# The prologue of a fused attention, delta-rule and MLP block: p's products first, three input tiles begun as u arrives, the decay's small operations as a chain

## The chip, the core and the metric

The kernel runs on one core of one Trainium2 chip. Five engines have each a queue of their own and work it off in order: PE (TensorE, matmuls), DVE (VectorE), ACT (ScalarE), POOL (GpSimd) and SP (SyncE, which issues most DMAs). The metric is the device time of one execution in microseconds (us), the median of several.

## What is computed

One transformer block over 512 positions of width 1024, all in float32. The part that matters here is its start: the norm of `x`, the wide projection `proj`, the decay of the gated delta rule, and the product of `p` that is needed only at the end.

```python
def reference(x, p, ...):
    u = rmsnorm(h, pre_mix_norm[i])
    proj = jnp.einsum('btd,de->bte', u, w_in[i])
    (da_q, da_k, da_v, gdn_qkv, gdn_z, gdn_b, gdn_a, gate_a_in, gate_b_in) = jnp.split(proj, splits, axis=-1)
    ...
    beta = jax.nn.sigmoid(gdn_b)
    log_decay = -jnp.exp(gdn_a_log[i]) * jax.nn.softplus(gdn_a + gdn_dt_bias[i])
    o_b = gated_delta_rule(g_q, g_k, g_v, log_decay, beta)    # uses cumsum(log_decay) per chunk
    ...
    e = jnp.einsum('btp,pd->btd', p[i], w_ple[i]) * jax.nn.sigmoid(...)
    return h + rmsnorm(e, ple_norm[i])
```

## The kernel before

Everything lies with channels on the 128 partitions and the 512 positions along the free axis: `x` and `u` are 8 pieces (`KD`) of 128x512. A product is made in three passes from split operands: ACT casts a tile to its high half (`whi`, `u_hi`), DVE or POOL subtracts to get the low half (`wlo`, `u_lo`), and PE adds high times high, high times low and low times high. An output tile of 128 columns is thus 24 matmuls of 128x512: 16 that use `whi` (with `u_hi[k]` and `u_lo[k]` in turn, `dense_steps`), and 8 with `wlo`. Here they are called the 16 and the lows.

**Prologue** (L170 to L199). `p` and two weights of `wple` are loaded, then `x` in 8 pieces. Squares of `x` (ACT, L182) are added up (DVE, L184), `norm_bc` makes the broadcast norm `psr` of the sum with small matmuls, a chain of small DVE operations and one matmul (L145 to L153), and the loop at L188 makes `u`: a scaled piece `ut` (DVE), `u_hi` (ACT), `u_lo` (DVE). The products of `p` are written behind it: 8 tiles of 6 matmuls, each copied from PSUM by ACT (`pp`, L197, two buffers) and sent to DRAM (`pp_d`, L198).

**Decay** (`scalars`, from L215). The tile `ba` holds the 32 columns of beta and decay; `pst` is its transpose, then about twenty operations on 128x64 tiles follow on DVE (`sy`, `sz`, `sp`: softplus by a series) up to `sg`, the log decay. The matmuls `psc` and `psg` sum it along time. `gcr` goes to DRAM and is read back broadcast over the partitions as `dt` (L428).

**Tiles of the projection** (`fill`). A list of output tiles in fixed order: for head 0 the key tile K, the query tile P, the value tiles V0 and V1, then `aq`, `ak`, `av`. Each loads its weights two tiles ahead (three buffers `raw`, two `whi`, two `wlo`). K, P, V0 and V1 go through a convolution (`conv_silu`: ACT, three `acc` operations on DVE at L372, ACT, one more on DVE).

**What sets the order.** Up to L829 a list scheduler orders the instructions of all engines. From `tc.manual_schedule` on, PE's order is that of the program text, which `run` lays out: steps of hand-written chains (`gdn_a`, `gdn_i`, `attn`, ...) are put between the matmuls of `fill`; a chain yields the microseconds of PE work that are to pass before its next step. The other engines are still ordered by the scheduler, with priorities per chain (`URGENT`). An engine waits at the head of its queue until that instruction's operands and buffers are ready. PSUM has three buffers `ps` for output tiles.

Of the kernel before, what the change touches and what calls it, by code (L numbers as in the profile page):

```python
# [37 lines left out]
def hybrid_block(ctx, tc, xT, pT, w1, wba, wa, wb, wo, wup, wdn, wple, wpg, vecs, rows, consts, out):  # L38
# [130 lines left out]

    with pool_("pro", bufs=2) as pool:  # L170
# [15 lines left out]
        for k in range(KD):  # L186
            t = pool.tile([128, T], F32, name="ut")
            V.scalar_tensor_tensor(t, in0=psr, scalar=vec[:, G_MIX + k:G_MIX + k + 1], in1=x[:, k], op0=mult, op1=mult)  # L188
            split(u[0][k], u[1][k], t, V)
        ph = pool.tile([128, 2, T], F32R, name="p_hi", bufs=1)  # L190
        pl = pool.tile([128, 2, T], F32R, name="p_lo", bufs=1)
        split(ph, pl, pr)
        p2 = act(ph), act(pl)
        for d in range(KD):
            ps = newdense(wple[d], p2, 2, G, raw=raws[d] if d < 2 else None)
            pp = pool.tile([128, T], F32, name="pp")
            S.activation(pp, ps, AF.Copy, scale=0.5)  # L197
            nc.sync.dma_start(pp_d[d], pp)  # L198
        nc.sync.dma_start(row, rows.partition_broadcast(128))  # L199
# [15 lines left out]
    def scalars():  # L215
        with pool_("sct", bufs=1) as pool:
            raw = wpool.tile([128, KD, 32], F32, name="ba_raw", tag="raw", bufs=3)
            nc.sync.dma_start(raw, wba)
            wz = [wpool.tile([128, KD, 128], F32R, name="ba_" + n, tag=n) for n in ("whi", "wlo")]
            for w in wz:  # L220
                G.memset(w.bitcast(F32), 0.0)
            split(wz[0][:, :, :32], wz[1][:, :, :32], raw)
            ps = pd.tile([128, T], F32, name="ps")
            dense(ps, wz, u, KD)
            ba = pool.tile([128, T], F32, name="ba")
            S.copy(ba[:32], ps[:32])
            th = pool.tile([16, T], F32, name="th16")
            S.activation(th, ba[:16], AF.Tanh, scale=0.5)
            V.tensor_scalar(th, th, 0.5, 0.5, op0=mult, op1=add)
            nc.sync.dma_start(ber_d, th)  # L230

            pst = pb.tile([128, NC, 32], F32, name="pst", tag="b")
            for c in range(NC):
                PE.matmul(pst[:, c], lhsT=ba[:32, c * 128:(c + 1) * 128], rhs=ident[:32, :32], is_transpose=True)
            S.activation(beta, pst[:, :, 0:16], AF.Tanh, scale=0.5)
            V.tensor_scalar(beta, beta, 0.5, 0.5, op0=mult, op1=add)
            shp = [128, NC, NH]
            y, e, z, z2, p, g = (pool.tile(shp, F32, name=n) for n in ("sy", "se", "sz", "sz2", "sp", "sg"))
            V.tensor_tensor(y, pst[:, :, 16:32], bc(row[:, 0:16], shp, 1), op=add)
            S.activation(e, y, AF.Abs)  # L240
            S.activation(e, e, AF.Exp, scale=-1.0)

            V.tensor_scalar(z, e, 2.0, None, op0=add)
            V.reciprocal(z, z)
            V.tensor_tensor(z, z, e, op=mult)
            V.tensor_tensor(z2, z, z, op=mult)
            V.tensor_scalar(p, z2, 1.0 / 19.0, None, op0=mult)
            for n in (17, 15, 13, 11, 9, 7, 5, 3):
                V.scalar_tensor_tensor(p, in0=p, scalar=1.0 / n, in1=z2, op0=add, op1=mult)
            V.scalar_tensor_tensor(p, in0=p, scalar=1.0, in1=z, op0=add, op1=mult)  # L250
            V.tensor_scalar(y, y, 0.0, None, op0=mx)
            V.scalar_tensor_tensor(y, in0=p, scalar=2.0, in1=y, op0=mult, op1=add)
            ea = pool.tile([128, 16], F32, name="ea")
            S.activation(ea, row[:, 16:32], AF.Exp)
            V.scalar_tensor_tensor(g, in0=y, scalar=-1.0, in1=bc(ea, shp, 1), op0=mult, op1=mult)

            gf = g.rearrange("p c h -> p (c h)")
            psc = pb.tile([128, 2, NC, NH], F32, name="psc", tag="b")
            PE.matmul(psc[:, 0].rearrange("p c h -> p (c h)"), lhsT=tri, rhs=gf, start=True, stop=True)
            PE.matmul(psc[:, 1].rearrange("p c h -> p (c h)"), lhsT=ones, rhs=gf, start=True, stop=True)  # L260
            S.copy(gc_t, psc[:, 0])
            S.activation(eg, psc[:, 0], AF.Exp)
            S.activation(egl, psc[:, 1], AF.Exp)
            V.scalar_tensor_tensor(nbeg, in0=eg, scalar=-1.0, in1=beta, op0=mult, op1=mult)
            V.tensor_tensor(edec, psc[:, 1], gc_t, op=sub)
            S.activation(edec, edec, AF.Exp)
            psg = pb.tile([128, T], F32, name="psg", tag="b")
            for c in range(NC):
                PE.matmul(psg[:16, c * 128:(c + 1) * 128], lhsT=g[:, c], rhs=tri, start=True, stop=True)
            gcr = pool.tile([16, T], F32, name="gcr")  # L270
            S.copy(gcr, psg[:16])
            nc.sync.dma_start(gcr_d, gcr)

            ltmp = pool.tile([128, 64], F32, name="ltmp")
            ls = pool.tile([128, 2], F32, name="ls")
            for i in range(2):
                o = 32 + 128 * i
                V.tensor_tensor(ltmp, row[:, o:o + 64], row[:, o + 64:o + 128], op=mult)
                V.tensor_reduce(ls[:, i:i + 1], ltmp, axis=AX.X, op=add)
            S.activation(ls, ls, AF.Exp)  # L280
            V.scalar_tensor_tensor(nlam, in0=ls[:, 1:2], scalar=-lam0, in1=ls[:, 0:1], op0=add, op1=sub)
# [819 lines left out]
```

## Time and profile before

| | us |
|---|---|
| median of 3 runs (1388.82 to 1392.7) | 1390.83 |
| the profiled execution | 1397.38 |
| its span in the profile | 1395.6 |
| PE busy | 1326.7 (95%) |
| DVE busy | 838.1 (60%) |
| ACT busy | 662.3 (47%) |

The span is one execution as the hardware profiler saw it on the core; the profiled execution's own time stands 6.6 us above the median of the timed runs. The page gives busy times for the whole span, so a stage has to be read from the timeline and from windows of it. A matmul's end is modelled, so the distance between the starts of two matmuls tells their rate better than their durations.

### The profile page before, as it was taken

Reading aid. Unit: us, or ns where it says so; the run is one execution under the profiler, and the core shown is the slowest. Engines: PE = TensorE matmul, PEld = TensorE weight load, DVE = VectorE, ACT = ScalarE, POOL = GpSimd, SP = SyncE. Lnnn points to the kernel's source line nnn. Section 1 sums busy time; section 2 is a strip of 40 time slices with the busy share of each in tenths; the row PEclk is TensorE's granted clock in tenths of the full one; section 3 lists DMA queues with packets and bytes.
Section 4 is the critical chain, followed back from the end, with each engine's and each line's share of the span. In section 5 each row is a group of like instructions: output and inputs, shape, how many; then the busy total and the mean of one; then the engine's idle time right before and its main releaser. Section 6 shows DMA issues by size and latency. Waiting matters only on the chain.

```text
span 1395.6 us, 22459 instructions
## 1 busy us (share of the span) xinstructions
PE 1326.7 (95%) x8402; PEld 1107.5 (79%) x8402; DVE 838.1 (60%) x2155; ACT 662.3 (47%) x1363; POOL 184.5 (13%) x193
## 2 busy tenths in 40 slices
PE   6989999999999999999999999999999999999986
PEld 4867787787777778878888888898888888888985
DVE  6867688777778768776653534368343224433575
ACT  5556575767667476766453412254232223223241
POOL 3111111101111111110000000003320002210341
PEclk9989999999999999999999999999999999999998
DMA  7466655655665566655354743351232233223321
GB/s 249 134 153 132 154 122 135 157 150 126 162 158 139 134 134 166 149 135 143 117 185 167 249 143 113 101 186 46 67 100 91 91 94 102 91 91 108 112 84 61
DMA packets 91117, 182.58 MB, mean 131 GB/s; under 512 B 33632, under 2 KB 40160, under 8 KB 91008
## 3 DMA queue, kind: packets, MB, share of 16 engines
q1 hardware_dynamic: 81648, 147.07, 33.6%
q0 software_dynamic: 9360, 34.08, 13.2%
q8 instruction: 66, 1.08, 0.3%
q14 instruction: 43, 0.35, 0.1%
HBM read 130.19 MB, written 16.84 MB: 105 GB/s over the span
## 4 chain that ended last, share of the span: by engine, by line
PE 73%; DVE 14%; DMA 6%; ACT 3%; SPq 2%; issue 2%; POOL 0%; DVEq 0%; ACTq 0%; POOLq 0%
PE ps L80 64%; DMA dt<-gcr_d 2%; DVE Uq L507 1%; SPq L474 1%; PE psat L80 1%; DVE tmpq L506 1%; DVE h L881 1%; PE psao L80 1%; DMA L<-ld_d 1%; DVE ht L880 1%; DVE acc L372 1%; DMA U<-ud_d 1%; PE psS L80 1%; PE psx L80 1%; DVE nw_t L93 1%
## 5 line engine op out<-in xcount | busy, mean ns | idle before, releaser
L80 PE MATMUL ps<-u_hi,whi 128*128 128x512 f32 (+1 forms) x952 | 385.0, 405 | 0.0
L80 PE MATMUL ps<-u_lo,whi 128*128 128x512 f32 (+1 forms) x952 | 374.8, 395 | 0.0
L80 PE MATMUL ps<-u_hi,wlo 128*128 128x512 f32 (+1 forms) x952 | 250.1, 396 | 0.0
L98 ACT CAST whi<-raw 128x1024 fp32r<-128x1024 f32 (+1 forms) x116 | 116.4, 1005 | 265.4 <-PE ps L80 258.5
L80 PEld LDWEIGHTS ps<-u_hi,whi 128*128 128x128 f32 x952 | 183.2, 192 | 35.4
L80 PEld LDWEIGHTS ps<-u_lo,whi 128*128 128x128 f32 x952 | 183.4, 193 | 33.9
L99 DVE TENSOR_TENSOR wlo<-raw,whi 128x1024 fp32r<-128x1024 f32 x106 | 130.1, 1227 | 126.5 <-PE ps L80 104.2
L80 PEld LDWEIGHTS ps<-u_hi,wlo 128*128 128x128 f32 x952 | 172.6, 189 | 33.7 <-issue 0.2
L117 POOL DMA_DIRECT2D wlo<-raw x65 | 56.2, 864 | 424.5 <-ACT wlo L116 224.6
L80 PE MATMUL ps<-hid_hi,whi 128*128 128x512 f32 x224 | 88.5, 395 | 0.0
L80 PE MATMUL ps<-hid_lo,whi 128*128 128x512 f32 x224 | 88.4, 394 | 0.0
L80 PE MATMUL ps<-brl,whi 128*128 128x512 f32 x208 | 82.1, 394 | 0.0
L80 PE MATMUL ps<-brh,whi 128*128 128x512 f32 x208 | 82.0, 395 | 0.0
L372 DVE SCALAR_TENSOR_TENSOR acc<-ps,cw,acc 128x511 f32<-128x511 f32 (+2 forms) x96 | 71.3, 743 | 8.5 <-ACT acc L369 7.7
L115 ACT CAST whi<-raw 128x1024 fp32r<-128x1024 f32 x65 | 68.0, 1046 | 17.3 <-PE ps L80 17.0
L116 ACT ACTIVATE wlo<-whi 128x1024 fp32r<-128x1024 f32 x65 | 68.6, 1056 | 0.3
L942 POOL TENSOR_TENSOR mr<-mr 128x512 f32<-128x512 f32 (+1 forms) x37 | 39.5, 1070 | 217.9 <-ACT hid_hi L941 217.2
L940 DVE SCALAR_TENSOR_TENSOR mr<-ps,r 128x512 f32<-128x512 f32 (+1 forms) x37 | 22.9, 619 | 74.4 <-PE ps L80 70.7
L80 PE MATMUL ps<-hid_hi,wlo 128*128 128x512 f32 x224 | 56.9, 395 | 0.0
L80 PE MATMUL ps<-brh,wlo 128*128 128x512 f32 x208 | 52.6, 395 | 0.0
L80 PEld LDWEIGHTS ps<-hid_lo,whi 128*128 128x128 f32 x224 | 42.1, 188 | 10.3
L80 PEld LDWEIGHTS ps<-hid_hi,wlo 128*128 128x128 f32 x224 | 42.0, 188 | 10.2
(334 smaller groups left out, 2425.4 us busy)
## 6 DMA issues: line engine op xcount, KB each, us to landing
raw<-w SPq DMA_DIRECT2D x88, 512.0 KB, 3.5
wlo<-raw POOLq DMA_DIRECT2D x65, 512.0 KB, 4.8
...
dt<-gcr_d SPq DMA_DIRECT2D x16, 256.0 KB, 5.1
bB<-ber_d SPq DMA_DIRECT2D x16, 256.0 KB, 5.2
ob_d<-zs SPq DMA_DIRECT2D x16, 256.0 KB, 3.0
```

The lines of the kernel that those rows point to most:

```text
L80: PE.matmul(ps, lhsT=lhsT, rhs=rhs, start=start, stop=stop, **k)
L93: V.tensor_tensor(t, t, h, op=mult)
L98: S.copy(hi, src)
L99: (eng or V).tensor_tensor(lo, src, hi.bitcast(F32), op=sub)
L115: S.copy(whi, raw)
L116: S.activation(wlo, whi.bitcast(F32), AF.Copy, scale=-1.0)
L117: nc.gpsimd.dma_start(wlo, raw, accum_op=add)
L372: V.scalar_tensor_tensor(acc[:, s:], in0=ps[:, :T - s], scalar=cw[:, j, w:w + 1], in1=acc[:, s:], op0=mult, op1=add)
L474: nc.sync.dma_start(dst, Bf[bs, :, bs])
L506: V.tensor_tensor(tv, bc(L[:, j, j + 1:], [128, m, r], 1), bc(Uq[:, :m, j], [128, m, r], 2), op=mult)
L940: V.scalar_tensor_tensor(r[:, :n], in0=ps[:, :n], scalar=0.0, in1=r2[:, sl], op0=mx, op1=mult)
L942: G.tensor_tensor(r[:, :n], r[:, :n], r[:, :n], op=mult)
```

## The change

The prologue is rewritten, and PE's manual order now begins at its top, so that PE follows the program text there too. Weights of `p` are loaded between the pieces of `x`; the products of `p` are placed ahead of the norm (d 0 and 1), ahead of its sum (2 to 4), inside `norm_bc` (5 and 6, by the new argument `between`) and behind it (7). Their low halves are made by DVE instead of POOL. The last square is not added by DVE but summed in PE. The weights of `ba`, K and P are loaded and cast in the prologue, and the loop over k gives each of the three tiles its two matmuls of the 16, the second tile one step of k behind the first, the third two. The lows of `ba` follow at once, those of K and P are given out by `fill` (`begun`, `lows`). `scalars` becomes a chain "C" of three steps with yields of 3 and 9, and its tiles lie in other buffers.

```diff
+    manual = tc.manual_schedule(engines={PE.engine})
+    manual.__enter__()
...
-        raws = [load_raw(wple[d], 2) for d in range(2)]
-        x = pool.tile([128, KD, T], F32, name="x", bufs=1)
-        for k in range(KD):
-            nc.sync.dma_start(x[:, k], xT[:, k])
+        load(0, 1)
+        load(0, 1, 2, wp=False)
+        load(2, 3)
+        load(3, 4, 5, wp=False)
+        load(4, 5)
+        load(6, 7, wp=False)
         nc.sync.dma_start(C, consts)
+        load(6, 7)
         nc.sync.dma_start(vec, vecs)
+        nc.sync.dma_start(ba_raw, wba)
+        firsts = [load_raw(w1[n], KD) for n in (24 + 8, 24)]
+        nc.sync.dma_start(row, rows.partition_broadcast(128))
...
+        def ple(*ds):
+            for d in ds:
+                w = [pool.tile([128, 2, 128], F32R, name="wp" + n, bufs=3) for n in "hl"]
+                split(*w, wr[:, d])
+                ps = pd.tile([128, T], F32, name="ps")
+                dense(ps, w, p2, 2)
+                pp = pool.tile([128, T], F32, name="pp")
+                S.activation(pp, ps, AF.Copy, scale=0.5)
+                nc.sync.dma_start(pp_d[d], pp)
+
+        ple(0, 1)
...
-            if k:
+            if 0 < k < KD - 1:
                 V.tensor_tensor(ss, ss, q, op=add)
-        psr = norm_bc(pool, pt, [ss], EPS)
+        ple(2, 3, 4)
+        psr = norm_bc(pool, pt, [ss, q], EPS, lambda: ple(5, 6))
+        ple(7)
+        S.copy(wz[0][:, :, :32], ba_raw)
+        ws = [wz]
+        for raw in firsts:
+            ws.append([...])
+            S.copy(ws[-1][0], raw)
+        begun = [pd.tile([128, T], F32, name="ps") for _ in ws]
+        for k in range(KD + 2):
+            if k < KD:
+                t = pool.tile([128, T], F32, name="ut")
+                V.scalar_tensor_tensor(t, in0=psr, scalar=vec[:, G_MIX + k:G_MIX + k + 1], in1=x[:, k], op0=mult, op1=mult)
+                split(u[0][k], u[1][k], t, V)
+            for n, (w, ps) in enumerate(zip(ws, begun)):
+                if 0 <= k - n < KD:
+                    for a in u:
+                        mm(ps, w[0][:, k - n], a[k - n], start=k == n and a is u[0], stop=False)
+        V.tensor_tensor(wz[1][:, :, :32], ba_raw, wz[0][:, :, :32].bitcast(F32), op=sub)
+        for raw, w in zip(firsts, ws[1:]):
+            V.tensor_tensor(w[1], raw, w[0].bitcast(F32), op=sub)
...
+    def scalars(_):
+        S.copy(ba[:32], begun[0][:32])
...
+        yield 3.0
+        pst = pb.tile([128, NC, 32], F32, name="pst", tag="b")
+        y, e, z, z2, p, g = (small[:, :, 16 * n:16 * n + 16] for n in range(6))
...
+        yield 9.0
+        PE.matmul(psc[:, 0], lhsT=tri, rhs=gf, start=True, stop=True)
...
+            if i < 2:
+                ps, steps = begun[i + 1], lows(i + 1)
...
+    chains.append([0.0, (), scalars, 0, ("C", 0)])
-        chains.append([0.0, (("V", h, 1), ("A", h - 1)), gdn_a, h, ("A", h)])
+        chains.append([0.0, (("V", h, 1), ("A", h - 1), ("C", 0)), gdn_a, h, ("A", h)])
```

Three places show how instructions move (in brackets what an instruction waits for; DMAHW is a DMA that has landed). On ACT, before, where `u` begins, the pieces of `u` alternate with the copies of p's products:

```order
L98 CAST whi2_274<-raw2_272 128x256 [waits DMAHW3_49,PE_49,Pool_49]
L98 CAST u_hi_90<-ut_160 128x512 [waits DVE_49]
L197 ACTIVATE pp_253<-ps_246 128x512 [waits DMAHW2_49,PE_49]
L98 CAST u_hi_90<-ut_164 128x512 [waits DVE_49]
L98 CAST whi2_290<-raw2_288 128x256 [waits DMAHW4_49,PE_49,Pool_49]
L98 CAST u_hi_90<-ut_168 128x512 [waits DVE_49]
```

Now, at the same place of ACT (`whi8_298` and `whi8_301` are K's and P's weights, `pp_195` to `pp_294` the copies of the products d 2 to 7):

```order
L231 CAST whi8_298<-raw8_121 128x1024 [waits DMAHW4_49]
L231 CAST whi8_301<-raw8_123 128x1024 [waits DMAHW5_49]
L214 ACTIVATE pp_195<-ps_188 128x512 [waits DMAHW7_49]
L214 ACTIVATE pp_209<-ps_202 128x512 [waits DMAHW0_49]
L214 ACTIVATE pp_223<-ps_216 128x512 [waits DMAHW2_49,PE_49,Activation_49]
L214 ACTIVATE pp_264<-ps_257 128x512 [waits DMAHW3_49,PE_49,Activation_49]
L214 ACTIVATE pp_278<-ps_271 128x512 [waits DMAHW5_49,PE_49,Activation_49]
L98 CAST u_hi_90<-ut_307 128x512 [waits DVE_49]
L214 ACTIVATE pp_294<-ps_287 128x512 [waits DMAHW6_49,PE_49,Activation_49]
L98 CAST u_hi_90<-ut_313 128x512 [waits DVE_49]
```

Five copies, each waiting for the write to DRAM of the copy two before it, now stand ahead of the first `u_hi`, and both weight casts ahead of them. On PE, before, `psc` stands in the lows of P (`ps_525`), the second tile of the projection:

```order
L80 MATMUL ps_525<-u_hi_90,wlo8_483 128x512 [waits DVE_49]
L80 MATMUL ps_525<-u_hi_90,wlo8_483 128x512 x5
L259 MATMUL psc_440<-sg_417,C_81 128x64 [waits DVE_49]
L260 MATMUL psc_440<-sg_417,ones_84 128x64
L269 MATMUL psg_449<-C_81,sg_417 16x128 [waits Activation_49]
L269 MATMUL psg_449<-C_81,sg_417 16x128 x3
```

Now it stands in V1 (`ps_563`), the fourth tile, behind 14 of its 16; `ps_626` is `aq`:

```order
L80 MATMUL ps_563<-u_lo_91,whi8_520 128x512
L308 MATMUL psc_578<-small_487,C_81 128x64 [waits DVE_49]
L309 MATMUL psc_578<-small_487,ones_84 128x64
L318 MATMUL psg_587<-C_81,small_487 16x128 [waits Activation_49]
L318 MATMUL psg_587<-C_81,small_487 16x128 x3
L80 MATMUL ps_563<-u_hi_90,whi8_520 128x512
L80 MATMUL ps_563<-u_lo_91,whi8_520 128x512
L80 MATMUL ps_563<-u_hi_90,wlo8_521 128x512 x8
L80 MATMUL ps_626<-u_hi_90,whi8_559 128x512 [waits Activation_49]
```

`psc` moved from the second tile to the fourth; from `aq` on, PE's order is the same as before to the end of the program. On DVE, before, the end of the decay's operations stands among the convolution of K (`acc_512`):

```order
L249 SCALAR_TENSOR_TENSOR sp_416<-sp_416,sz2_415 128x64 [waits DVE_49]
L372 SCALAR_TENSOR_TENSOR acc_512<-ps_486,cw_329,acc_512 128x510 [waits DVE_49]
L249 SCALAR_TENSOR_TENSOR sp_416<-sp_416,sz2_415 128x64 [waits DVE_49]
L372 SCALAR_TENSOR_TENSOR acc_512<-ps_486,cw_329,acc_512 128x509 [waits DVE_49]
L249 SCALAR_TENSOR_TENSOR sp_416<-sp_416,sz2_415 128x64 [waits DVE_49] x2
L250 SCALAR_TENSOR_TENSOR sp_416<-sp_416,sz_414 128x64 [waits DVE_49]
L252 SCALAR_TENSOR_TENSOR sy_412<-sp_416,sy_412 128x64 [waits DVE_49]
L255 SCALAR_TENSOR_TENSOR sg_417<-sy_412,ea_437 128x64 [waits DVE_49]
```

Now it stands among and behind that of V0 (`acc_550`), the third tile, and behind the low half of `aq`'s weights (`wlo8_560`); `small_487` holds all the decay's tiles, and L303 writes the log decay:

```order
L424 SCALAR_TENSOR_TENSOR acc_550<-ps_524,cw_406,acc_550 128x510 [waits DVE_49]
L297 SCALAR_TENSOR_TENSOR small_487<-small_487 128x4x16 [waits DVE_49]
L424 SCALAR_TENSOR_TENSOR acc_550<-ps_524,cw_406,acc_550 128x509 [waits DVE_49]
L297 SCALAR_TENSOR_TENSOR small_487<-small_487 128x4x16 [waits DVE_49]
L99 TENSOR_TENSOR wlo8_560<-raw8_557,whi8_559 128x1024 [waits DMAHW7_49,PE_49]
L297 SCALAR_TENSOR_TENSOR small_487<-small_487 128x4x16 [waits DVE_49]
L426 SCALAR_TENSOR_TENSOR vraw0_549<-vraw0_549,acc_550 128x512 [waits DMAHW3_49,DMAHW6_49,DMAHW1_49,Activation_49]
L297 SCALAR_TENSOR_TENSOR small_487<-small_487 128x4x16 [waits DVE_49]
L298 SCALAR_TENSOR_TENSOR small_487<-small_487 128x4x16 [waits DVE_49]
L300 SCALAR_TENSOR_TENSOR small_487<-small_487 128x4x16 [waits DVE_49]
L303 SCALAR_TENSOR_TENSOR small_487<-small_487 128x4x16 [waits DVE_49]
```

What moved is the last third of the decay's operations: from between K's convolution steps to between and behind those of V0.

## Rows read from the trace of the kernel before

**Rows 1.** Windows: busy us (PE, PEld, DVE, ACT, POOL), granted TensorE clock, DMA share, GB/s.
```profile
40.00:50.00 10.00, 10.00 (x50) 7.94 (x49) 8.80 (x25) 5.41 (x12) 0.00 (x0) 1.00 0.28 102
50.00:60.00 10.00, 10.00 (x45) 8.28 (x45) 8.17 (x14) 3.60 (x7) 1.51 (x1) 1.00 0.67 212
```
**Rows 2.** Chain of waits, two pieces: start, us, what.
```profile
27.62 2.10 DMA pp_d<-pp
...
48.87 12.01 PE ps L80 x52
```
**Rows 3.** Timeline of u's production: start, us, engine, line, operation [idle before <-releaser].
```profile
21.54 0.75 DVE L188 SCALAR_TENSOR_TENSOR ut<-psr,vec,x 128x512 f32<-128x512 f32 x1 [1.22 <-PE psr L153]
...
27.74 0.68 DVE L99 TENSOR_TENSOR u_lo<-ut,u_hi 128x512 fp32r<-128x512 f32 x1
...
29.13 0.68 DVE L99 TENSOR_TENSOR u_lo<-ut,u_hi 128x512 fp32r<-128x512 f32 x1
...
30.22 0.50 PE L80 MATMUL ps<-u_hi,ba_whi 128*128 128x512 f32 x1 [2.19 <-ACT ba_whi L98]
...
35.07 0.50 PE L80 MATMUL ps<-u_lo,ba_whi 128*128 128x512 f32 x1
```
**Rows 4.** DMA issues of four short stretches: KB each, us from issue to landing.
```profile
x<-xT SPq DMA_DIRECT2D x1, 256.0 KB, 7.0
...
raw<-wple SPq DMA_DIRECT2D x1, 128.0 KB, 4.8
...
pp_d<-pp SPq DMA_DIRECT2D x1, 256.0 KB, 2.0
...
pp_d<-pp SPq DMA_DIRECT2D x1, 256.0 KB, 4.0
```
**Rows 5.** Issues of the last x (its line: ns min/median/max, first to last) and of that weight.
```profile
L176 SPq DMA_DIRECT2D x<-xT x8: 431/432/923, 2.1 to 5.4; - x8
...
9.04 0.33 SPq L106 DMA_DIRECT2D raw<-wple  x1
```
**Rows 6.** Timeline of DVE and PE around the end of the decay's operations.
```profile
42.40 1.23 DVE L99 TENSOR_TENSOR wlo<-raw,whi 128x1024 fp32r<-128x1024 f32 x1
...
43.55 0.22 DVE L249 SCALAR_TENSOR_TENSOR sp<-sp,sz 128x64 f32<-128x64 f32 x1
43.68 0.74 DVE L372 SCALAR_TENSOR_TENSOR acc<-ps,cw,acc 128x511 f32<-128x511 f32 x1
...
44.34 0.21 DVE L249 SCALAR_TENSOR_TENSOR sp<-sp,sz 128x64 f32<-128x64 f32 x1
...
46.95 0.23 DVE L255 SCALAR_TENSOR_TENSOR sg<-sy,ea 128x64 f32<-128x64 f32 x1
...
47.23 0.43 PE L259 MATMUL psc<-sg,C 128*128 128x64 f32 x2
...
48.80 0.73 PE L80 MATMUL ps<-u_hi,wlo 128*128 128x512 f32 x2
```
**Rows 7.** Timeline: psk in aq, the second bB of head 0, the first psx.
```profile
60.72 0.60 PE L80 MATMUL psk<-C,kq 128*128 128x128 f32 x4
...
62.90 1.29 POOL L433 TENSOR_TENSOR bB<-bB,dt 128x512 f32<-128x512 f32 x1 [1.42 <-ACT dt L432]
...
70.75 0.28 PE L80 MATMUL psx<-kqh 128*128 128x256 f32 x1
```
**Rows 8.** Timeline of PE behind a wait of 3.47 us.
```profile
99.10 0.80 PE L80 MATMUL psao<-vt,aT 128*128 128x128 f32 x2 [3.47 <-ACT aT L736]
...
100.55 0.63 PE L80 MATMUL ps<-u_hi,whi 128*128 128x512 f32 x1
100.97 0.63 PE L80 MATMUL ps<-u_lo,whi 128*128 128x512 f32 x1
```
**Rows 9.** Windows around that wait, columns as in rows 1.
```profile
98.00:100.00 2.00, 0.90 (x3) 0.90 (x4) 1.90 (x9) 2.00 (x4) 0.00 (x0) 0.50 0.23 86
...
104.00:106.00 2.00, 2.00 (x12) 1.74 (x11) 1.00 (x4) 0.29 (x1) 0.00 (x0) 0.93 0.71 131
```

More of the change, by code (lines that the diff above doesn't have):

```diff
@@ L136, in dense_steps, with norm_bc @@
                 yield
-    def norm_bc(pool, pp, sss, eps):
+    def norm_bc(pool, pp, sss, eps, between=None):
         n = sss[0].shape[1] // 128
@@ L151, in norm_bc @@
         V.tensor_tensor(dg, bc(ident, [128, n, 128], 1), bc(r, [128, n, 128], 2), op=mult)
+        if between:
+            between()
         psr = pp.tile([128, 128 * n], F32, name="psr", tag="t")
@@ L167, in hybrid_block, with load @@
     u = (act(upool.tile([128, KD, T], F32R, name="u_hi")), act(upool.tile([128, KD, T], F32R, name="u_lo")))
+    manual = tc.manual_schedule(engines={PE.engine})
+    manual.__enter__()
+    begun = []
     with pool_("pro", bufs=2) as pool:
         pr = pool.tile([128, 2, T], F32, name="pr", bufs=1)
[L172 to L176 removed]
+        x = pool.tile([128, KD, T], F32, name="x", bufs=1)
+        wr = pool.tile([128, KD, 2, 128], F32, name="wr", bufs=1)
+        def load(*ds, wp=True):
+            for d in ds:
+                nc.sync.dma_start(wr[:, d] if wp else x[:, d], wple[d] if wp else xT[:, d])
+        nc.sync.dma_start(pr, pT)
+        load(0, 1)
[4 more added lines that the diff above has]
+        load(6, 7, wp=False)
         nc.sync.dma_start(C, consts)
+        load(6, 7)
         nc.sync.dma_start(vec, vecs)
+        ba_raw = wpool.tile([128, KD, 32], F32, name="ba_raw", tag="raw", bufs=3)
+        nc.sync.dma_start(ba_raw, wba)
+        firsts = [load_raw(w1[n], KD) for n in (24 + 8, 24)]
+        nc.sync.dma_start(row, rows.partition_broadcast(128))
+        wz = [pool.tile([128, KD, 128], F32R, name="ba_" + n, bufs=1) for n in "hl"]
+        for w in wz:
+            G.memset(w.bitcast(F32), 0.0)
+        ph = pool.tile([128, 2, T], F32R, name="p_hi", bufs=1)
+        pl = pool.tile([128, 2, T], F32R, name="p_lo", bufs=1)
+        split(ph, pl, pr)
+        p2 = act(ph), act(pl)
+        def ple(*ds):
+            for d in ds:
+                w = [pool.tile([128, 2, 128], F32R, name="wp" + n, bufs=3) for n in "hl"]
[6 more added lines that the diff above has]
+        ple(0, 1)
         ss = pool.tile([128, T], F32, name="ss", bufs=1)
@@ L182, in hybrid_block, with lows @@
             S.activation(q, x[:, k], AF.Square)
-            if k:
+            if 0 < k < KD - 1:
                 V.tensor_tensor(ss, ss, q, op=add)
-        psr = norm_bc(pool, pt, [ss], EPS)
[L186 to L199, printed above, removed]
+        ple(2, 3, 4)
[4 more added lines that the diff above has]
+        for raw in firsts:
+            ws.append([wpool.tile([128, KD, 128], F32R, name=f"w{n}{KD}", tag="w" + n) for n in ("hi", "lo")])
+            S.copy(ws[-1][0], raw)
[12 more added lines that the diff above has]
+            V.tensor_tensor(w[1], raw, w[0].bitcast(F32), op=sub)
+        def lows(n):
+            for k in range(KD):
+                mm(begun[n], ws[n][1][:, k], u[0][k], start=False, stop=k == KD - 1)
+                if k % 2:
+                    yield
+        for _ in lows(0):
+            pass
     NH = 16
@@ L213, in hybrid_block @@
     ber_d = dram.tile([NH, T], F32, name="ber_d")
[L215 to L281, printed above, removed]
@@ L304, in hybrid_block @@
     apool = apool_.__enter__()
-    scalars()
     gpool_ = pool_("ga", bufs=1)
@@ L341, in fill @@
                 yield tuple(after)
-            for j in range(i, min(i + 2, len(units))):
+            for j in range(max(i, 2), min(i + 2, len(units))):
                 if j not in ws:
                     ws[j] = load_w(units[j][1], KD, units[j][2])
-            ps = pd.tile([128, T], F32, name="ps")
-            for _ in dense_steps(ps, ws.pop(i), u, KD):
+            if i < 2:
+                ps, steps = begun[i + 1], lows(i + 1)
+            else:
+                ps = pd.tile([128, T], F32, name="ps")
+                steps = dense_steps(ps, ws.pop(i), u, KD)
+            for _ in steps:
                 yield ()
```

54 lines of the change are left out of this document (51 added, 3 removed).

## The prediction

> **What bounds the kernel now.** I read the windows first, then the chain of waits, then the timeline ahead of the full stretch. From 40 to 60 us PE is busy in all of the time [rows 1], and the chain runs there through its matmuls: 52 of them in 12.01 us, one per 0.23 [rows 2]. Ahead of it u is the bound. It is made from 21.54 on, one piece per 1.39 us (u_lo starts at 27.74 and 29.13); ba's first matmul starts at 30.22, the one that takes the last piece of u at 35.07 [rows 3]. So two things set the time here: when u is ready, and how many matmuls are then left. The reader is to see a third: in the PE-bound stretch DVE is busy 8.80 and 8.17 of 10 us [rows 1]. What has to pass DVE there has little room.
>
> **What the change removes.** Before, 20 of the 72 matmuls of ba, K and P have begun when u is complete, so 52 are left. Now the loop feeds all three tiles; with the last piece of u 11 of the 48 are left (1 of ba, 4 of K, 6 of P) and the 24 lows: 35. That is 17 x 0.23 = 3.9 us, if u is ready at the same time and nothing waits. The products of p cost PE nothing on the path in either version: it has idle time ahead of u. DVE makes p's low halves in place of POOL while it waits for x. x itself lands later, by the 0.52 MB of weights now ahead of its last piece; at the rate worked out below that is 1.4 us, and it is hidden, since something else is later still.
>
> **When u is ready.** ACT's order decides. Ahead of the first u_hi stand the casts of K's and P's weights and five copies pp. The last piece of x, the end of 2.89 MB, was issued at 5.4 [rows 5] and landed 7.0 later, at 12.4; a weight of p, the end of 3.43 MB, was issued at 9.04 [rows 5] and landed 4.8 later, at 13.84 [rows 4]. That is 0.38 MB per us. P's weights are now the end of 5.26 MB: 12.4 + 2.37 / 0.38 = 18.6, and cast at 19.7. Then the copies, 0.6 each: they have two buffers, so the third waits until the write of the first has landed, and the fifth for the write of the third. That ACT stands still for such a write is on the chain before too, with 2.10 us [rows 2]. A write takes 2.0 us alone and 4.0 behind a 512 KB load [rows 4], and loads of that size (V0's and V1's weights) are now issued between the writes. So u_hi begins at 19.7 + 0.6 + (2.0 to 4.0) + 0.6 + (2.0 to 4.0) + 0.6 = 25.5 to 29.5; I take the middle, 27.5, as both kinds of write occur. The first u_hi, one more copy and the second u_hi end at 29.4, then comes a u_lo every 1.39 us, the last two back to back: done at 37.8, with bounds 35.8 and 39.8. Before it was 35.0. The psr matmul is no later: PE needs the second copy for its seventh product of p, and that with psr behind it ends near 25 (27 at half the rate).
>
> The Trainium skill, page "DMA: Bandwidth & Descriptors", section "Anatomy of one DMA — SWDGE (gpsimd) path", says that a DMA signals only when its last byte is confirmed in the target memory, and fits 2.0 us plus the bytes over 436 GB/s. By this page an estimate for a write of 262 KB is 2.6 us, and with it u would be ready 0.8 us earlier than I take. The rows have 2.0 and 4.0 on the queue that is used here, and they decide.
>
> **PE up to psc.** Behind u stand 35 matmuls, pst (0.4), V0's 24 and 14 of V1: 73 x 0.23 + 0.4 = 17.2, so PE arrives at psc at 55.0. The count holds before: 102 matmuls, pst and 1.6 for psc and psg make 25.5 from 35.07 to psk, and psk starts at 60.72, 25.65 later [rows 7].
>
> **The wait that is added.** psc needs the log decay, and PE's order has nothing that it may take first; all later matmuls queue behind it. On DVE the log decay now stands behind the convolutions of K, P and V0, the low halves of V0's, V1's and aq's weights and four products. That queue starts when K's lows have been used (27 matmuls behind u, at 44.0), since V0's low half takes their buffer. I take distances between starts, as steps of DVE overlap a little [rows 6]: a low half 1.15 (42.40 to 43.55), a step of a convolution 0.66 (43.68 to 44.34), a small operation between others 0.13 (43.55 to 43.68), one that waits for its predecessor some 0.25. Three low halves make 3.45, nine steps 5.95, four products of some 0.6 2.4, 14 small ones 1.8, the reciprocal 0.5, four dependent ones at the end 1.0, waits for ACT 0.5: 15.6. The log decay is ready at 59.6, and PE waits 4.6. Lower bound: DVE has caught up when V0 is complete at 51.8; ACT's step and the DVE steps behind it take 6.1 more: 57.9, a wait of 2.9. Upper: nothing overlaps, 2.0 more, a wait of 6.6.
>
> **The clock behind it.** After a wait of 3.47 us that ends at 99.10 the granted clock is 0.50, which is the level of 1.2 GHz, and matmuls start 0.42 apart (100.55, 100.97) [rows 8]; at 104 to 106 it is at 0.93 [rows 9]. Five microseconds at half the rate lose some 2.4. I take 2.0, as psc and psg are short; bounds 0 and 2.4.
>
> **The sum.** Behind the log decay come psc and psg, 1.6 (47.23 to 48.80 [rows 6]), ten matmuls of V1, 2.3, and the clock, 2.0: aq begins at 65.5, where it was 60.3 (two matmuls ahead of psk). In terms: u +2.7, fewer matmuls -3.9, wait +4.6, clock +2.0, together +5.4; by the times +5.2. With all bounds low aq begins at 35.8 + 20.1 + 3.9 = 59.8, -0.5; with all high at 39.8 + 23.8 + 3.9 + 2.4 = 69.9, +9.6. From aq on PE's order is the same in both versions to the end, and the later waits hang on PE's own progress, so I carry the difference whole. The profiled execution of before took 1397.4 with a span of 1395.6; its sum would be 1402.7. It stands 6.6 above the median of the timed runs, which is what is predicted: 1390.8 + 5.3 = **1396.1 us**.
>
> **Rival 1: it does what it says.** The yields of 3 and 9 us are enough and PE does not wait at psc. aq begins at 37.8 + 17.2 + 3.9 = 58.9, -1.4, and with u as early as before at 56.1, -4.2: 1386.6 to 1389.4, say 1388. For it: before, the decay took 8.9 us from pst to the log decay. Against it: the DVE steps that now stand between. It decides from a DVE queue under 11 us instead of 15.6.
>
> **Rival 2: not slower.** u at its early bound, DVE near its lower bound, and a clock that does not fall: 35.8 + 21 + 3.9 = 60.7, +0.4, so 1391 to 1392. For it: short writes of 2.0 us [rows 4]. Against it: the clock [rows 8, 9]. It decides where the wait stays under 3 us and u is done by 36.
>
> **Rival 3: a second wait.** From the log decay to the second bB, through DRAM and back, it took 64.2 - 47.2 = 17.0 us before [rows 6, 7], and psx at 70.75 left 6.5 to spare. Now the first psx comes 16.6 behind the log decay: nothing to spare but some 2 us up to the second psx, which waits for what DVE makes of bB. A read slower by 2 to 5 us adds as much: +7 to +11, 1400. For it: in a full queue a load took 7.0 [rows 4]. Against it: the queue is emptier here.
>
> **How the numbers follow.** Forecast 0.57, rival 1 0.08, rival 2 0.20, rival 3 0.15. A measurement can tell about 0.3%, 4.2 us, from no change. Of the forecast's spread (-0.5 to +9.6, most of it +2.5 to +8) some seven tenths lie above +4.2: slower 0.40 + 0.15 = 0.55. Rival 2, the rest of the forecast and half of rival 1 are within: 0.41. Faster 0.04. The range leaves out most of rival 1 and the end of rival 3: 1390 to 1402.
>
> **What would show it.** Right: one wait of PE of 3 to 7 us at psc, released by DVE; the granted clock near 0.5 behind it; ACT standing still between copies ahead of the first u_hi; the last u_lo at 36 to 40; psk at 63 to 69; the waits of before at 90 to 100, shifted and not smaller. Wrong: no wait at psc (rival 1), one at psx (rival 3), u done by 35, or later waits that shrink by what was lost, so that the end does not move.

## The result and the profile after

The changed kernel takes 1402.45 us (median of four runs, 1401.93 to 1406.16), beside 1391.76 for the kernel before. The ratio is 1.0072, with a 95% interval of 1.0048 to 1.0096: slower by about 10 us. Run again beside three experiments it gave 1.0076 (1.0051 to 1.0101).

The waits of PE are read first. They are summed by what they waited for, for the first 140 us of the changed kernel (us in total, times, longest):

```profile
PE ps L80 <- ACT wph L98: 5.9, 1, 5.9
PE psc L308 <- DVE small L303: 5.0, 1, 5.0
PE psao L80 <- ACT aT L788: 4.4, 1, 4.4
PE ps L80 <- ACT pp L214: 4.2, 1, 4.2
...
PE psx L80 <- DVE intra L518: 0.6, 1, 0.6
```

The first is at the very start, for the first weights of p. The second is the new wait at psc. The third is the wait of before at psao [rows 8], now 4.4. The fourth is PE waiting for a copy of p's products, ahead of u. The last is a new wait at psx, the place that rival 3 names.

Windows of the changed kernel, columns as in [rows 1]:

```profile
40.00:50.00 10.00, 10.00 (x47) 7.96 (x46) 4.18 (x9) 5.23 (x10) 0.57 (x1) 1.00 0.20 44
50.00:60.00 10.00, 6.83 (x31) 5.32 (x29) 10.00 (x23) 4.58 (x7) 1.28 (x1) 1.00 0.62 222
60.00:70.00 10.00, 8.18 (x32) 6.27 (x33) 4.45 (x16) 3.61 (x11) 0.00 (x0) 0.66 0.32 105
...
62.00:64.00 2.00, 2.00 (x10) 1.56 (x11) 0.62 (x4) 0.71 (x4) 0.00 (x0) 0.50 0.42 166
```

PE was full from 40 to 60 [rows 1]. Now DVE is full from 50 to 60 and PE is not, and from 62 on PE works at a granted clock of 0.50, the level of 1.2 GHz. The same place in the timeline (start, us, engine, line, operation, idle before it and what ended that):

```profile
58.91 1.21 DVE L99 TENSOR_TENSOR wlo<-raw,whi 128x1024 fp32r<-128x1024 f32 x1
...
60.18 0.68 DVE L426 SCALAR_TENSOR_TENSOR vraw<-vraw,acc 128x512 f32<-128x512 f32 x1
...
61.55 0.22 DVE L303 SCALAR_TENSOR_TENSOR small<-small 128x64 f32<-128x64 f32 x1
...
61.82 0.69 PE L308 MATMUL psc<-small,C 128*128 128x64 f32 x2 [4.99 <-DVE small L303]
...
65.71 2.78 PE L80 MATMUL ps<-u_hi,wlo 128*128 128x512 f32 x8
...
68.79 0.60 PE L80 MATMUL psk<-C,kq 128*128 128x128 f32 x4
```

A low half and a step of V0's convolution run on DVE just ahead of the log decay, and PE stands for 4.99 us. psk starts at 68.79; it was at 60.72 [rows 7]. These 8.1 us are some four fifths of the loss of about 10.

How u came to be late shows on ACT, in the order of its queue:

```profile
19.39 1.04 ACT L231 CAST whi<-raw 128x1024 fp32r<-128x1024 f32 x1 [0.22 <-DMA raw<-w]
20.40 1.23 ACT L214 ACTIVATE pp<-ps 128x512 f32<-128x512 f32 x2
23.96 0.60 ACT L214 ACTIVATE pp<-ps 128x512 f32<-128x512 f32 x1 [2.33 <-DMA pp_d<-pp]
25.07 0.60 ACT L214 ACTIVATE pp<-ps 128x512 f32<-128x512 f32 x1 [0.52 <-DMA pp_d<-pp]
27.63 0.60 ACT L214 ACTIVATE pp<-ps 128x512 f32<-128x512 f32 x1 [1.96 <-DMA pp_d<-pp]
28.21 0.62 ACT L98 CAST u_hi<-ut 128x512 fp32r<-128x512 f32 x1
```

Between the copies ACT stands still for the writes, three times. The first u_hi starts at 28.21, behind the fifth copy. The end of u, on DVE and on PE:

```profile
37.18 1.46 DVE L99 TENSOR_TENSOR u_lo<-ut,u_hi 128x512 fp32r<-128x512 f32 x2
...
39.43 0.39 PE L80 MATMUL ps<-u_lo,ba_h 128*128 128x512 f32 x1
```

u is complete at 38.64, and ba's matmul with its last piece starts at 39.43; before, it was at 35.07 [rows 3].

### The profile page after: what moved, and what is told of

It reads as the page before. It is cut to its first block, busy times and chain, and to the rows that moved or that the text cites. A ratio compares the mean times of both kernels' runs of the same rounds, so it can differ in the third digit from the quotient of the medians.

```text
span 1401.2 us, 22459 instructions
## 1 busy us (share of the span) xinstructions
PE 1327.4 (95%) x8410; PEld 1105.0 (79%) x8410; DVE 836.2 (60%) x2162; ACT 660.2 (47%) x1363; POOL 178.5 (13%) x185
## 4 chain that ended last, share of the span: by engine, by line
PE 72%; DVE 14%; DMA 7%; ACT 2%; SPq 2%; issue 2%; DVEq 0%; ACTq 0%
PE ps L80 63%; DMA L<-ld_d 1%; DMA dt<-gcr_d 1%; SPq L526 1%; DVE Uq L559 1%; PE psat L80 1%; DMA U<-ud_d 1%; DVE acc L424 1%; DVE tmpq L558 1%; DVE h L932 1%; PE psao L80 1%; DVE ht L931 1%; PE psS L80 1%; DMA raw<-w 1%; PE psV L80 1%
## 5 line engine op out<-in xcount | busy, mean ns | idle before, releaser
L80 PE MATMUL ps<-u_hi,whi 128*128 128x512 f32 (+1 forms) x952 | 381.0, 401 | 0.0
L80 PE MATMUL ps<-u_lo,whi 128*128 128x512 f32 (+1 forms) x952 | 370.7, 391 | 0.0
L98 ACT CAST whi<-raw 128x1024 fp32r<-128x1024 f32 x106 | 111.0, 1049 | 252.1 <-PE ps L80 249.6
L99 DVE TENSOR_TENSOR wlo<-raw,whi 128x1024 fp32r<-128x1024 f32 x104 | 126.9, 1220 | 126.9 <-PE ps L80 104.6
L115 ACT CAST whi<-raw 128x1024 fp32r<-128x1024 f32 x65 | 67.9, 1044 | 12.8 <-PE ps L80 12.7
L993 POOL TENSOR_TENSOR mr<-mr 128x512 f32<-128x512 f32 (+1 forms) x37 | 39.5, 1068 | 216.5 <-ACT hid_hi L992 215.7
```

Of the source, the lines that this page charges most:

```text
L80: PE.matmul(ps, lhsT=lhsT, rhs=rhs, start=start, stop=stop, **k)
L98: S.copy(hi, src)
L99: (eng or V).tensor_tensor(lo, src, hi.bitcast(F32), op=sub)
L115: S.copy(whi, raw)
L993: G.tensor_tensor(r[:, :n], r[:, :n], r[:, :n], op=mult)
```

## The experiments

All ratios are to the kernel before. The three columns of times come from one profiled execution each: when u is complete, how long from there to psk, and when psao starts, the matmul behind the wait of [rows 8].

| kernel | u complete | u to psk | psao | ratio |
|---|---|---|---|---|
| before | 35.0 | 25.7 | 99.1 | 1 |
| before, again | 34.1 | 25.7 | 98.3 | |
| changed | 38.6 | 30.2 | 108.3 | 1.0072 |
| changed, again (e9) | 39.3 | 30.2 | 109.3 | 1.0076 |
| e1 eight pp | 34.1 | 29.9 | 104.3 | 1.0048 |
| e2 lows on POOL | 39.3 | 29.8 | 109.6 | 1.0075 |
| e3 filled wait | 39.0 | 27.9 | 107.4 | 1.0080 |
| e4 = e1 + e2 | 34.1 | 29.3 | 103.4 | 1.0046 |
| e6 decay early, psc late | 40.4 | 23.1 | 102.2 | 1.0013 |
| e7 = e6 + e1 | 34.1 | 23.1 | 96.1 | 0.9986 |
| e8 = e7, only ba in the loop | 34.3 | 29.3 | 103.5 | 1.0035 |
| e10 decay early | 39.2 | 25.9 | 104.0 | 1.0044 |
| e11 psc late | 39.8 | 26.9 | 106.4 | 1.0057 |
| e12 = e7 + P's low on POOL | 34.6 | 23.1 | 96.5 | 0.9985 |

Each interval is 0.12 to 0.25% wide to either side.

**e1, eight buffers for the copies.** Takes away what ACT waits for.

```diff
-                pp = pool.tile([128, T], F32, name="pp")
+                pp = pool.tile([128, T], F32, name="pp", bufs=8)
```

> One edit of the changed kernel: the copies pp of p's products get eight buffers in place of two, so no copy waits for the write to DRAM of an earlier one. Theory (the copies hold u, directly and through PE): in the changed kernel PE waits 4.2 us for a copy ahead of the fifth product, and psr stands behind the sixth; the casts of K's and P's weights end at 20.4, so with free buffers products 5 and 6 follow at once and the first u_hi begins near 25.6 in place of 28.2. u is complete 2.6 us earlier; the wait at psc (5.0) and the low clock behind it stay, as DVE's queue moves along. psk near 66.2 in place of 68.8, 0.2% faster than the changed kernel. Rival (PE's rate): products 5 and 6 run at half rate anyway, psr ends where it did, and nothing moves: psk at 68 to 69. Rival (DVE alone sets it): u is earlier but log decay is not, the wait at psc grows to 7 or 8, psk stays at 68.8.

u is complete 4.5 us earlier, as early as before; the two waits (ACT's for the writes and PE's for the copies) had held psr as well, which now starts at 20.84 in place of 26.34. The wait at psc stays, 4.9. The ratio is 1.0048 (1.0031 to 1.0065). So the copies do hold u, by more than expected; that DVE alone sets the time fails, since the log decay came earlier along with u.

**e2, low halves of head 0 on POOL.**

```diff
-        return "dma" if h else V
+        return "dma" if h else G
```

> One edit of the changed kernel: the low halves of head 0's weights (V0, V1, aq, ak, av) are made by POOL in place of DVE; POOL does nothing from 41 to 56 us. Theory (the length of DVE's queue sets the wait at psc): three low halves of 1.15 us each leave the queue between 45.9 and 61.8, so log decay is ready at 58.3 and PE, which arrives at 56.8, waits 1.5 in place of 5.0; with a wait that short the clock may stay up, which gives back up to 2.7 more. psk at 62.6 to 65.3 in place of 68.8; the whole 3.5 to 6.2 us, 0.25 to 0.45%, faster than the changed kernel. Rival (latency of the dependent small operations sets it, not what stands between them): the wait stays at 4 to 5 us, psk at 68 to 69. Rival (POOL is too slow: 2.4 us for such a tile in the kernel before): PE waits for a low half of V0, V1 or aq instead, or the second psx waits for bB, which POOL makes too, and the total does not move.

The wait at psc is 4.3, the ratio 1.0075 (1.0054 to 1.0095): nothing gained. The wait is near what the latency rival gave, but for another reason. Two rows of POOL, and the two operations of the decay on DVE (a group's line: count, ns min/median/max, first and last start) that overlap them:

```profile
56.96 1.32 POOL L99 TENSOR_TENSOR kql<-kq,kqh 128x512 fp32r<-128x512 f32 x1 [5.57 <-ACT kqh L98]
58.23 2.34 POOL L99 TENSOR_TENSOR wlo<-raw,whi 128x1024 fp32r<-128x1024 f32 x1
```

```profile
L297 DVE SCALAR_TENSOR_TENSOR small<-small x2: 1182/1724/2265, 57.2 to 58.4; 128x64 f32<-128x64 f32 x2
```

One operation took 1.18 and one 2.27 us, where the others of the same line take 0.21 to 0.23; each ended some 0.1 us behind POOL's. Another (L291), which has a single input, took 1.40 in place of 0.18 beside an earlier low half on POOL. Together that is 4.2 us, more than the 3.45 taken off the queue; counted from u the log decay is 0.7 earlier all the same, and the wait is shorter by that. The Trainium skill, page "SBUF — State Buffer", section "SBUF: two separate sides", has a rule for this: DVE and GpSimd share one pair of ports, which the one that starts first keeps for its whole instruction, and a DVE operation with two inputs in SBUF is blocked by a GpSimd operation that reads SBUF. The trace agrees for the operations of L297, which have two inputs in SBUF; the convolution's steps, with one input in PSUM, kept their 0.73 us. L291, with its single input, is not covered by this part of the rule.

**e3, the wait filled with work.** Sixteen matmuls that nobody reads, ahead of psc.

```diff
         gf = g
+        psd = pb.tile([128, T], F32, name="psd", tag="b")
+        for i in range(16):
+            PE.matmul(psd, lhsT=ws[1][0][:, i % 8], rhs=u[0][i % 8], start=i == 0, stop=i == 15)
```

> Sixteen matmuls of 128x512, whose result nobody reads, are put on PE just ahead of psc of the changed kernel: 3.6 us of work in the place of most of the wait of 5.0. The edit also moves log decay ahead of the low half of aq on DVE, so it is ready some 1.2 earlier, near 60.6; the matmuls end at 60.4. Theory (the wait costs twice, as a wait and by the low clock behind it): no wait over 1 us at psc, granted clock near 1 behind it, and from the first psc matmul to the first of psk 4.3 us in place of 7.0; psk at 64.9 to 65.3 in place of 68.8, the whole some 3.6 us, 0.26%, faster than the changed kernel although PE does more. Rival (the clock behind psc is low for another reason, or psc to psk is long for the matmuls' own dependence): psc to psk stays near 7, psk at 67.6.

```profile
62.53 0.41 PE L311 MATMUL psc<-small,C 128*128 128x64 f32 x2 [0.51 <-DVE small L303]
...
64.64 2.00 PE L80 MATMUL ps<-u_hi,wlo 128*128 128x512 f32 x8
...
66.93 0.60 PE L80 MATMUL psk<-C,kq 128*128 128x128 f32 x4
```

From psc to psk it is now 4.40 us, where the changed kernel needs 6.97: eight matmuls take 2.00 in place of 2.78. The low clock behind the wait costs 2.57. The log decay was not earlier but 0.6 later than in the changed kernel (u was 0.3 later), so that part of the expectation failed. In the whole nothing is gained: 1.0080 (1.0060 to 1.0101). psao starts only 0.9 earlier than in the changed kernel although psk is 1.9 earlier, and the total, known to 0.2%, cannot show so little.

**e4, both.** The edits of e1 and e2.

> Both edits of the two runs before together (eight buffers pp, low halves of head 0 on POOL). Theory: the gains add, u 2.6 earlier, the wait at psc 1.5 or less, the clock up behind it: psk at 60 to 62.7, against 60.7 in the kernel before and 68.8 in the changed one. The whole 6 to 9 us faster than the changed kernel, level with the kernel before or up to 0.1% off either way. Rival (the two overlap: an earlier PE only waits longer for DVE): the wait at psc is 3 to 4 us and psk at 65.

psk at 63.4, the wait at psc 4.3, the ratio 1.0046 (1.0031 to 1.0062): what e1 gives, and no more, as e2 alone would have it.

**e5, the kernel before a second time.** No edit.

> The kernel before, unchanged, profiled a second time, since its first profiled execution took 6.6 us more than the median of its runs and four landmarks of it are compared with all others: the first matmul of psk (60.7), of psq of the second and third head (118.8, 201.0) and of the last head (607.3). Theory (the loss of the change is made by psk, and the extra time of that execution lies behind): psk again at 60 to 61.5, and the later landmarks earlier than in the first profile by as much as this execution is faster. Rival (the prologue itself varies by some us): psk moves by more than 1.5 us, and then differences of that size between single profiles of the other kernels mean nothing either.

It took 1393.58, 3.8 less than the first. psk is at 59.8, u complete 0.9 earlier, and from u to psk it is 25.7 again. So u moves by about a microsecond between executions, and the distance from u to psk does not. The later landmarks are earlier by 0.8, 0.6 and 2.3 (118.0, 200.4, 605.0): the extra time of the first profile lay mostly behind the first heads.

**e6, decay early and psc late.** Two numbers.

```diff
-        yield 3.0
+        yield 0.0
         pst = pb.tile([128, NC, 32], F32, name="pst", tag="b")
...
-        yield 9.0
+        yield 15.0
         gf = g
```

> The changed kernel with the two yields of the decay chain at 0 and 15 in place of 3 and 9: the transposes pst come right behind the lows of ba, some 3.3 us earlier, and psc stands behind V1 and two matmuls of aq, with psk right behind it. PE then arrives at psc at 56.8 + 2.75 = 59.6; log decay is ready between 58.5 (the whole 3.3 earlier) and 61.1 (DVE's queue is full from 45.9 on, only the last step of V0's convolution is now behind it). Theory (psc is placed too early for DVE): a wait of 0 to 1.5 us in place of 5.0, no stretch of low clock, psk at 61.2 to 64 in place of 68.8, and the whole 5 to 7 us, 0.35 to 0.5%, faster than the changed kernel. Rival (what is won at psk is lost again behind it, where between 90 and 110 us loads and writes keep the DMA engines busy and PE waits for aT): psk as above, but the wait at psao grows from 4.4 to 6 or more, and the whole is at most 3 us faster.

The ratio is 1.0013 (1.0000 to 1.0027), some 8 us faster than the changed kernel. PE's row has no wait, and psk follows 1.6 behind psc:

```profile
61.92 0.43 PE L308 MATMUL psc<-small,C 128*128 128x64 f32 x2
...
63.49 0.66 PE L80 MATMUL psk<-C,kq 128*128 128x128 f32 x4
```

u happened to be complete 1.8 later than in the changed kernel, and psk is still 5.3 earlier. The rival fails: the wait at psao fell to 2.9.

**e7, the same with eight buffers.**

> The edit of the run before and the eight buffers pp together. With eight buffers u was complete at 34.1 (38.6 in the changed kernel, 35.0 before) and PE would be at psc at 52.3 + 2.75 = 55.1; log decay at 53.9 to 56.6. Theory: no wait over 1.5 us, psk at 56.7 to 59.5, against 60.7 before; carried to the end that is 9 to 12 us less than the changed kernel and 1 to 4 us, 0.1 to 0.3%, less than the kernel before. Rival (given back behind psk): psk as above, the wait at psao 6 to 8 us, and the whole between the two kernels, 2 to 5 us over the kernel before.

psk at 57.2, the ratio 0.9986 (0.9975 to 0.9998): 2 us faster than the kernel before, with an interval that just leaves out no change, and about 12 us faster than the changed kernel. Against e6 the eight buffers are worth 0.27%. The rival fails here too; the wait at psao is 4.1.

**e8, only ba in the loop.** As e7, with the change's three tiles undone.

```diff
-            for n, (w, ps) in enumerate(zip(ws, begun)):
+            for n, (w, ps) in enumerate(zip(ws[:1], begun)):
...
         def lows(n):
+            for k in range(KD if n else 0):
+                for a in u:
+                    mm(begun[n], ws[n][0][:, k], a[k], start=k == 0 and a is u[0], stop=False)
+                yield
```

> As the run before, but the loop over u feeds only ba, as in the kernel before; K and P take all of their 16 behind it. Behind the last piece of u 1 + 8 + 48 = 57 matmuls are left in place of 35, and PE stands idle in the loop. Theory (a begun tile is worth its matmuls): 22 x 0.227 = 5.0 us more from u's last piece to psk, psk 5.0 later than in the run before, 61.7 to 64.5, and no wait at psc, since the decay now starts ahead of the convolutions. Rival (PE in the loop was not free, or the decay's wait is what counts): the distance from u to psk grows by under 3 us.

From u to psk it is 29.3, 6.2 more than in e7, and the ratio is 1.0035 (1.0023 to 1.0047), 0.49% above e7. So begun tiles are worth their 22 x 0.227 = 5.0 us, and 1.2 more. Two rows of e8 show where that is, a window in the loop and the one in which u ends, and below them those of e7:

```profile
26.00:30.00 4.00, 2.48 (x7) 1.12 (x6) 3.90 (x6) 1.86 (x3) 2.38 (x5) 0.80 0.98 339
...
34.00:36.00 2.00, 2.00 (x6) 1.44 (x6) 0.40 (x2) 0.00 (x0) 0.00 (x0) 0.50 0.03 8
```

```profile
26.00:30.00 4.00, 3.42 (x13) 2.17 (x13) 3.90 (x7) 1.90 (x4) 2.82 (x6) 1.00 0.99 356
...
34.00:36.00 2.00, 2.00 (x10) 1.62 (x9) 0.22 (x2) 0.00 (x0) 0.00 (x0) 1.00 0.00 0
```

With one tile in the loop PE is idle for 1.5 of the 4 us from 26 on, and its granted clock is 0.50 when u is complete; with three it is idle for 0.6, and the clock is 1.00. The eight lows of ba, which come next, take 3.62 us in e8 and 2.03 in e7.

**e9, the changed kernel again,** beside e10 to e12.

> The changed kernel as it is, beside the other three on one chip. Both theories: the ratio to the kernel before inside the interval measured first (1.0048 to 1.0096), u complete at 38 to 41, the wait at psc 4 to 5 us, psk 68 to 71. It serves as the base for the two runs that take the two edits of the sixth run apart.

Ratio 1.0076, the wait at psc 5.0, from u to psk 30.2: all as in the first run.

**e10, decay early only.**

```diff
-        yield 3.0
+        yield 0.0
...
-        yield 9.0
+        yield 12.5
```

> Yields of 0 and 12.5: pst comes right behind the lows of ba, psc stays where it is in the changed kernel, with ten matmuls of V1 behind it. In the sixth run log decay was ready 21.5 us behind the last piece of u, in the changed kernel 23.1. Theory (two things add: DVE's start and PE's place): log decay 1.6 earlier, the wait at psc 3.4 in place of 5.0, the clock behind it still low; psk about 1.6 earlier than in the changed kernel, counted from u, and the whole 0.1% faster. Rival (the early start was all of the gain of the sixth run): the wait under 1 us, psk 5 us or more earlier, the whole 0.4 to 0.6% faster.

The log decay comes 21.4 behind u in place of 23.1, as expected, but the wait is 2.6 and not 3.4, since PE's way to psc has a wait of 0.7 at pst now. And the clock stays up behind it, which was not expected. The wait, and the windows around it:

```profile
60.63 0.43 PE L308 MATMUL psc<-small,C 128*128 128x64 f32 x2 [2.59 <-DVE small L303]
...
65.05 0.60 PE L80 MATMUL psk<-C,kq 128*128 128x128 f32 x4
```

```profile
58.00:60.00 2.00, 0.04 (x1) 0.00 (x0) 2.00 (x5) 0.00 (x0) 0.91 (x1) 1.00 0.14 55
...
62.00:64.00 2.00, 2.00 (x11) 1.51 (x9) 1.36 (x6) 1.70 (x4) 0.00 (x0) 1.00 0.52 182
```

From u to psk it is 4.2 less than in the changed kernel, the ratio 1.0044 (1.0025 to 1.0063): between the two expectations.

**e11, psc late only.**

```diff
-        yield 9.0
+        yield 12.0
```

> Yields of 3 and 12: pst where it is in the changed kernel, psc behind V1 and two matmuls of aq, as in the sixth run. DVE's order puts the last three small operations between the steps of V1's convolution, so log decay comes up to 2.2 us later, 23.1 to 25.3 behind u. PE comes to psc 2.75 later. Theory (the wait only moves along with DVE's queue): a wait of 2.2 to 4.5 us, the clock low behind it, psk 0.5 to 2.8 us earlier than in the changed kernel, counted from u; the whole 0 to 0.2% faster. Rival (the place of psc was all of the gain of the sixth run): the wait under 1 us, psk 5 us or more earlier, the whole 0.4 to 0.6% faster.

The log decay is 24.8 behind u, the wait 3.9, the clock 0.50 in the window from 66 to 68. From u to psk it is 3.2 less than in the changed kernel, a little more than the theory's 2.8, but here a part of the low clock lies behind psk and is not in that distance: V1 stands ahead of psc, so only 2.1 us pass from psc to psk.

```profile
66.77 1.11 PE L80 MATMUL psk<-C,kq 128*128 128x128 f32 x4
```

```profile
66.00:68.00 2.00, 2.00 (x9) 1.52 (x8) 1.47 (x6) 0.85 (x3) 0.00 (x0) 0.50 0.62 180
68.00:70.00 2.00, 2.00 (x8) 1.53 (x8) 0.55 (x6) 1.94 (x10) 0.00 (x0) 0.75 0.29 107
```

From psk to psq, the next transpose on PE, it takes 5.65 in e11 and 4.55 to 4.64 in every other kernel. Counted from u to psq e11 is 2.1 earlier than the changed kernel, inside the theory's range, e10 4.2 and e6 7.0. The ratio is 1.0057 (1.0035 to 1.0079). Neither edit is the whole of e6: 2.1 + 4.2 = 6.3.

**e12, P's low half on POOL.** As e7, with one more edit.

```diff
-        for raw, w in zip(firsts, ws[1:]):
-            V.tensor_tensor(w[1], raw, w[0].bitcast(F32), op=sub)
+        for raw, w, eng in zip(firsts, ws[1:], (V, G)):
+            eng.tensor_tensor(w[1], raw, w[0].bitcast(F32), op=sub)
```

> The seventh run with one more edit: the low half of P's weights is made by POOL (2.4 us, while DVE makes pieces of u) in place of DVE, where it stands between the second ut and the first u_lo (23.30, 1.22 us). Theory: u is complete 1.2 us earlier, 32.9 in place of 34.1, psk 1.2 earlier, 56.0, the whole some 1 us faster than in the seventh run, which is at the limit of what can be told. Rival (as in the second run, where a small DVE operation beside such a POOL operation took 2.27 us in place of 0.21): operations of DVE on pieces of u stand still while POOL works, u is no earlier or up to 1.2 later.

No gain, 0.9985 (0.9969 to 1.0001). POOL's row, and beside it the first u_lo and the second:

```profile
22.62 2.39 POOL L244 TENSOR_TENSOR wlo<-raw,whi 128x1024 fp32r<-128x1024 f32 x1 [20.04 <-ACT whi L231]
```

```profile
24.12 1.43 DVE L99 TENSOR_TENSOR u_lo<-ut,u_hi 128x512 fp32r<-128x512 f32 x1
...
26.26 0.68 DVE L99 TENSOR_TENSOR u_lo<-ut,u_hi 128x512 fp32r<-128x512 f32 x1
```

The first u_lo, with two inputs in SBUF, took 1.43 in place of 0.68, until POOL was done at 25.0; the ut ahead of it, which reads psr from PSUM, took its 0.74. The norm ahead of it was 0.7 later in this execution, so that u was complete 0.6 later than in e7 and not earlier. Counted from the first ut, u took 11.95 us in place of 12.10: 0.15 is left of the 1.2 that was expected.

## Why the prediction was right, and where it was short

The forecast was slower, 1396.1 with a range to 1402; the median lies 0.45 above the range. The ratio of 1.0072, taken on the 1390.83 from which the forecast starts, makes 1400.8, inside it. The forecast added 5.3 us and some 10 were measured, so the size was off by about half. The mechanism was the forecast's: one wait at psc that DVE releases, low clock behind it, copies that hold u. e1, e6, e7 and e10 show it by taking it away. No errors cancelled: u, the wait, the clock and what lies behind psk all came out larger than forecast.

- **u.** Forecast +2.7, measured +4.4 for PE (39.43 against 35.07). The casts ended at 20.43 and not at 19.7. The two writes were taken at 3.0 each. From their issue to the start of the copy that waits it took 2.9 (21.02 to 23.96) and 3.1 (24.58 to 27.63), and the medians of the four issues are 3.1 and 2.7 (next fence), so the middle was right. The prediction's estimate of 2.6, from the fit on the Trainium skill's page "DMA: Bandwidth & Descriptors", section "Anatomy of one DMA — SWDGE (gpsimd) path", was a little low. The step that failed is the end: I took PE to be at the last piece when u is complete. Three tiles are 6 matmuls per piece, 6 x 0.23 = 1.38 us. Up to the seventh piece, one per 1.39, PE is at most 0.2 behind; the last two u_lo come back to back, 0.7 apart, and PE reaches the last piece 0.8 after it is done. That the norm is no later than the copies held only just: psr ended at 27.40, above the forecast's 25 and its 27 at half the rate, and the first ut behind it (27.43, 0.75 us) was ready as the fifth copy ended.

The landings of the writes, issued from 19 to 22 and from 24 to 27 us:

```profile
pp_d<-pp SPq DMA_DIRECT2D x2, 256.0 KB, 3.1
```

```profile
pp_d<-pp SPq DMA_DIRECT2D x2, 256.0 KB, 2.7
```

- **Fewer matmuls.** Forecast -3.9 by the count. PE came to psc 17.4 behind its last-piece matmul, 17.2 in the forecast; e8 tests the worth of begun tiles by itself.
- **The wait.** Forecast 4.6, measured 5.0. The log decay was 2.2 later than forecast, and PE 1.8. DVE's queue itself was well priced, at 15.6: from V0's low half (45.86) to the log decay (61.77) it took 15.9.
- **The clock.** Forecast 2.0 and at most 2.4; e3 and e10 give 2.57 and 2.55. The term was too small: psg and the first matmuls of V1 all ran at 0.50. I took less than 2.4 because psc and psg are short, but from psc to V1's next matmul it took 2.87 in place of 1.57 [rows 6].
- **Rival 3.** Its sign came, a wait of 0.65 at psx where it priced 2 to 5, but not its cause. The read was not slower: the second bB ended at 77.16, 15.4 behind the log decay, where it took 17.0 before. DVE began to work on psx and bB only at 81.94. Two of the operations ahead of that in its queue stood still beside POOL's work on bB:

```profile
74.31 2.85 POOL L485 TENSOR_TENSOR bB<-bB,dt 128x512 f32<-128x512 f32 x2 [16.98 <-ACT dt L484]
```

```profile
74.67 1.26 DVE L501 TENSOR_TENSOR edr<-edec,r2k 128x8 f32<-128x8 f32 x1
75.92 1.26 DVE L90 TENSOR_SCALAR nw_h<-gss 128x4 f32<-128x4 f32 x1
```

In e10 the same two took 0.17 and 0.16, as bB came after them, and PE did not wait for DVE at psx.

- **The sum.** At psk 4.4 - 3.9 + 5.0 + 2.6 = 8.1, as measured, where 5.3 was forecast. Against the second profile of before (e5) it is 9.0.
- **What lies behind psk.** I carried the difference whole. It grew: psao starts 9.2 later than in the first profile of before, and 10.1 later than in the second. Of the 1.1 to 1.2 that is added between psk and psao, 0.9 has arisen when psv starts, the first transpose behind psx (18.8 behind psk in place of 17.9): that is where the wait at psx lies. The table shows that psao is the better place to read: over all kernels its shift against the mean of the two profiles of before (98.7), divided by 1393, gives the ratio to within 0.18%, for eight of the twelve ratios to within 0.06%. What releases psao in the changed kernel is a chain of waits (start, us, what):

```profile
97.48 5.22 DMA wlo<-raw
...
102.75 4.36 DMA raw<-w
107.11 0.86 ACT whi L115
...
108.03 0.26 ACT aT L788
...
108.34 0.79 PE psao L80 x2
```

aT stands on ACT behind a weight cast, which waits for a load (raw) that SP issued when the transfer ahead of it (wlo) had landed. From psk to psao it took 38.4 and 38.5 in the two profiles of before, 38.7 to 39.0 in e6, e7, e10 and e12, and 39.5 to 40.5 in all others. Four of the five runs with an early pst are the short ones (e8 is the fifth). Up to psv the traces say why: PE waits for DVE at psx for at most 0.2 us in these four and for 0.5 to 1.3 in the others; e11 has no such wait, but 1.1 of low clock there. From psv to psao it takes 20.4 to 20.8 in the four and 20.6 to 21.5 in the others; what sets that part, DVE's order or the loads', stays open.
